# Second FFN of a two-block kernel in two phases, with the up product of a gate and value pair in seven block products

## The chip, the cores and the metric

The kernel runs on one core of a Trainium2 chip. Times are device microseconds of one execution; the median of three runs of the kernel before is 2676.65 us (2674.63 to 2678.04). The engines are PE (TensorE), ACT (ScalarE), DVE (VectorE), POOL (GpSimd) and SP (SyncE, which issues DMAs in order); DMAs that the text calls POOL's are issued in order on POOL's queue.

## What is computed

Two transformer-like blocks run in sequence on x of 1024 tokens by 1024 channels, in float32. The change touches the FFN of the second block (and the loop ahead of it); d_ff is 2816, so the up product has 5632 columns.

```python
    x = x + merged @ w_out[l]
    h2 = _rmsnorm(x, norm2_g[l])
    up = _dwconv_centred(h2 @ w_up[l], ffn_dw_w[l], ffn_dw_b[l])
    gate, val = jnp.split(up, 2, axis=-1)
    x = x + (jax.nn.gelu(gate, approximate=False) * val) @ w_down[l]
return _rmsnorm(x, norm_f_g)
```

The depthwise convolution has three taps along the tokens.

## The kernel before

Activations lie as tiles of 128 channels by 1024 tokens. Each float32 operand is split into a rounded part hi and a rest lo (`split`: ACT makes hi, DVE subtracts), and each product of two tiles is three matmuls, hi by hi, hi by lo and lo by hi, of 128x512. Weights come by `w_prep` in the order of the list `seq`: SP loads wraw (512 KB), ACT makes whi, DVE wlo; there are two buffers of each. The matmuls of one 512-token half add up in one PSUM bank, a tile pg, and `evac` reads it.

**First FFN** (lines 140 to 214 and 806 to 850). Four units of the up product are plain, then `strassen` takes the units in pairs: with four factors T1 to T4 of the activations, made once by `factors`, a pair is 7 block products of 12 matmuls in place of 8 (84 matmuls for 96). `st_prep` makes the weight side of a pair: it loads the first unit as raw, the two halves of the second as U[1] and A, adds U[0] = U[1] + A on DVE, subtracts raw to get V and U[1] = raw - V, and splits S2, S1, S3, A22 and S4 into sh (ACT) and sl (DVE). `keep` copies a partial sum from PSUM to a tile abc on ACT, `ends` (on DVE) adds it to a bank and scales. The result goes to DRAM and is loaded again for the down product, a phase of its own.

**Second block.** In `merge` the eight out2 units (24 matmuls per half, two halves) make x2, DVE adds the residual, `split` makes h2, and `sumsq` adds squares on POOL (line 311). `stats_rB` sums them by two matmuls into pss (line 315) and makes rB, 1/rms per token. `block2_ffn` then runs up unit by up unit: `up(i)` makes the gate unit i and the value unit 22+i, each 48 matmuls, `evac` multiplies by rB on DVE (line 1008), and DVE does the convolution: middle tap and bias (line 1012), two outer taps (1013, 1014); ACT does gelu (1016), DVE the product (1017), and `split` makes the act. The 22 acts are taken in six groups `G2`; the down product of a group (`down`, line 750: x[m] += pg on DVE) runs after the first pairs of the next group. There are three PSUM banks for pg. The last group runs with the final norm.

The order on each engine is made by a scheduler from the program's order; pieces under `high_priority` go earlier, and a pool's buffers set who waits.

Of the kernel before, what the change touches and what calls it, by code (L numbers as in the profile page):

```python
# [57 lines left out]
LEAD, TRAIL = 4, 2  # L58


class Body:
# [694 lines left out]
    def block1_ffn(self):  # L756
        nc, A = self.nc, self.A
        H0, H1 = self.H0, self.H1
        with self.pool("o1") as o1:
# [46 lines left out]

            def factors(j):

                x, y = xr[j], xr[j + 4]
                for t, m in ((x, j), (y, j + 4)):  # L810
                    nc.scalar.activation(out=t, in_=t, func=AF.Copy, scale=self.vec("g_mlp", m))
                a, b = slice(0, HN), slice(HN, T)
# [593 lines left out]
```

## Time and profile before

| | us |
|---|---|
| median of 3 runs | 2676.65 |
| the profiled execution | 2674.9 |
| its span | 2673.1 |
| PE busy | 2619.5 (98%) |
| DVE busy | 1626.0 (61%) |
| ACT busy | 889.4 (33%) |
| POOL busy | 190.0 (7%) |

The granted clock of PE is 0.994 of full speed in the mean. The second FFN with its down product takes PE from about 1940 to 2615 us of the span; the block products of the first FFN stand from 603 to 868 us. The page divides the span into 40 slices of 67 us; the DMA engines are busy 1 to 3 tenths in most of them.

### The profile page before, as it was taken

What the parts mean: (1) busy time and instruction counts of PE and PEld (TensorE: products, weight loads), DVE (VectorE), ACT (ScalarE), POOL (GpSimd) and SP (SyncE); (2) the same over time, 40 slices, a digit from 0 to 9 for tenths busy, and PEclk for the clock granted to TensorE, in tenths of its full rate; (3) what the DMA queues carried; (4) which work ended last, traced back from release to release, by engine and by line L of the source; (5) the groups of instructions that cost most, each with busy time, mean ns of one, the idle gap of its engine ahead of it and who ended that gap; (6) DMA issues with size and microseconds to landing.
All of it is one profiled execution on the core that took longest, in us unless ns stands there. A gap on an engine that the chain in (4) does not pass through costs nothing. (4 is left out here: it accounts for less than half of the span.)

```text
span 2673.1 us, 31765 instructions
## 1 busy us (share of the span) xinstructions
PE 2619.5 (98%) x12844; PEld 2170.0 (81%) x12844; DVE 1626.0 (61%) x2242; ACT 889.4 (33%) x1307; POOL 190.0 (7%) x175
## 2 busy tenths in 40 slices
PE   8999998999999999999999999999999999999998
PEld 7888886877888888888877778887888888888887
DVE  8688688555655544445398777434566645555664
ACT  5455454334443212124344342413221111111121
POOL 1111111210000000003000000011200000000001
PEclk9999999999999999999999999999999999999999
DMA  3101111323333811124222211112211111111111
GB/s 136 44 29 44 40 44 64 133 99 100 120 101 122 319 49 54 48 97 140 79 82 69 68 49 50 47 49 70 96 40 48 52 51 48 48 48 48 48 63 64
DMA packets 77249, 200.33 MB, mean 75 GB/s; under 512 B 9568, under 2 KB 26288, under 8 KB 77104
## 3 DMA queue, kind: packets, MB, share of 16 engines
q1 hardware_dynamic: 63872, 168.34, 19.1%
q10 hardware_dynamic: 9216, 16.78, 1.7%
q0 software_dynamic: 4016, 13.19, 1.3%
q8 instruction: 101, 1.65, 0.3%
q14 instruction: 44, 0.36, 0.0%
HBM read 164.20 MB, written 34.08 MB: 74 GB/s over the span
## 5 line engine op out<-in xcount | busy, mean ns | idle before, releaser
L217 PE MATMUL pg<-hi,whi 128*128 128x512 f32 (+1 forms) x2576 | 1002.0, 389 | 2.6 <-ACT hi L278 1.9
L217 PE MATMUL pg<-lo,whi 128*128 128x512 f32 (+1 forms) x2576 | 999.2, 388 | 0.8 <-DVE lo L279 0.8
L217 PE MATMUL pg<-hi,wlo 128*128 128x512 f32 (+1 forms) x2576 | 999.0, 388 | 0.3 <-DVE wlo L120 0.3
L217 PEld LDWEIGHTS pg<-hi,whi 128*128 128x128 f32 x2576 | 484.6, 188 | 101.8 <-ACT hi L278 2.3
L217 PEld LDWEIGHTS pg<-lo,whi 128*128 128x128 f32 x2576 | 484.6, 188 | 99.0 <-issue 1.2
L217 PEld LDWEIGHTS pg<-hi,wlo 128*128 128x128 f32 x2576 | 484.6, 188 | 97.4 <-DVE wlo L120 0.8
L119 ACT ACTIVATE whi<-wraw 128x1024 fp32r<-128x1024 f32 x189 | 200.2, 1060 | 803.1 <-PE pg L217 669.5
L120 DVE TENSOR_TENSOR wlo<-wraw,whi 128x1024 fp32r<-128x1024 f32 x189 | 235.9, 1249 | 85.0 <-ACT whi L119 83.9
L750 DVE TENSOR_TENSOR xr<-xr,pg 128x512 f32<-128x512 f32 x128 | 87.4, 686 | 159.6 <-PE pg L217 159.6
L1008 DVE TENSOR_TENSOR u<-pg,rB 128x512 f32<-128x512 f32 x88 | 60.7, 690 | 176.2 <-PE pg L217 176.2
L1136 DVE SCALAR_TENSOR_TENSOR cv<-u,vecs,cv 128x1023 f32<-128x1023 f32 (+14 forms) x120 | 152.6, 1272 | 1.7
L243 PE MATMUL pg<-hi,whi 128*128 128x512 f32 x256 | 108.5, 424 | 0.0
L750 DVE TENSOR_TENSOR x<-x,pg 128x512 f32<-128x512 f32 x80 | 54.7, 686 | 86.7 <-PE pg L217 86.7
L160 PE MATMUL pg<-hi,sh 128*128 128x512 f32 x260 | 101.7, 391 | 4.1 <-ACT sh L145 4.1
L243 PE MATMUL pg<-hi,wlo 128*128 128x512 f32 x256 | 102.3, 400 | 0.0
L160 PE MATMUL pg<-hi,sl 128*128 128x512 f32 x260 | 101.9, 392 | 0.4 <-DVE sl L126 0.4
L243 PE MATMUL pg<-lo,whi 128*128 128x512 f32 x256 | 101.9, 398 | 0.0
L160 PE MATMUL pg<-lo,sh 128*128 128x512 f32 x260 | 101.7, 391 | 0.0
L278 ACT ACTIVATE hi<-c 128x1024 fp32r<-128x1024 f32 x22 | 23.3, 1061 | 128.0 <-DVE c L1017 128.0
L519 POOL TENSOR_TENSOR X<-bq,b 128x256 f32<-128x256 f32 x60 | 50.5, 855 | 210.3 <-DVE bq L519 93.7
L1268 PEld LDWEIGHTS pao<-V,pT 128*128 128x128 f32 x384 | 48.6, 191 | 20.2 <-ACT pT L1266 16.0
L575 PEld LDWEIGHTS psc<-X 128*128 128x128 f32 x480 | 59.3, 191 | 4.3 <-issue 1.4
(327 smaller groups left out, 3542.6 us busy)
## 6 DMA issues: line engine op xcount, KB each, us to landing
wraw<-w_up SPq DMA_DIRECT2D x63, 512.0 KB, 3.3
wraw<-w_dn SPq DMA_DIRECT2D x54, 512.0 KB, 3.3
wraw<-w_in SPq DMA_DIRECT2D x52, 512.0 KB, 3.4
ad<-r ACTq DMA_DIRECT2D x64, 256.0 KB, 2.1
r<-ad SPq DMA_DIRECT2D x32, 512.0 KB, 6.6
bt<-bias SPq DMA_DIRECT2D x48, 192.0 KB, 2.4
wraw<-w_out SPq DMA_DIRECT2D x16, 512.0 KB, 3.5
wraw<-w_v SPq DMA_DIRECT2D x10, 512.0 KB, 3.8
```

Source lines behind the costliest of these rows:

```text
L119: nc.scalar.activation(out=hi, in_=raw, func=AF.Copy)
L120: nc.vector.tensor_tensor(out=lo, in0=raw, in1=hi.bitcast(F32), op=ALU.subtract)
L160: nc.tensor.matmul(out=p, lhsT=a[:, k, :], rhs=b, start=first and k == 0 and j == 0, stop=k == 3 and j == 2, skip_group_check=True)
L217: nc.tensor.matmul(out=p, lhsT=w, rhs=x[:, hs], start=(i == 0 and j == 0), stop=(i == n - 1 and j == 2))
L243: nc.tensor.matmul(out=p, lhsT=w[:, k, :], rhs=x[:, hs], start=(k == 0 and j == 0), stop=(k == 7 and j == 2))
L278: nc.scalar.activation(out=hi, in_=src, func=AF.Copy)
L519: tt = lambda e, o, a, b, op: e.tensor_tensor(out=o, in0=a, in1=b, op=op)
L575: nc.tensor.matmul(out=ps[:, j, :], lhsT=lt[:, js], rhs=r, start=True, stop=True)
L750: nc.vector.tensor_tensor(out=xr[m][:, hs], in0=xr[m][:, hs], in1=p, op=ALU.add)
L1008: nc.vector.tensor_tensor(out=u[:, hs], in0=p, in1=self.rB[:, hs], op=ALU.mult)
L1136: nc.vector.scalar_tensor_tensor(out=c[:, o], in0=u[:, s], scalar=w(k), in1=c[:, o], op0=ALU.mult, op1=ALU.add)
L1268: nc.tensor.matmul(out=po[0][:, n, ps_], lhsT=pT[:, kt, :], rhs=V[h + kt][:, n, ps_], start=(kt == 0), stop=(kt == 2))
```

## The change

The eight out2 units run in the order 0, 4, 1, 5, ... (`PAIRED`), each stores its x2 to DRAM (x2d, tile xe) on POOL's queue. The second FFN becomes two phases. Up: three plain pairs (gate i and value 22+i), then pairs 3 to 20 by `strassen` with the gate as first and the value as second unit, then pair 21 plain inside strassen's `tail`. Each act goes to DRAM (ad2, tile ae) by SP. Down: all groups, with acts and x2 loaded again by SP. `factors` is a method now and makes T1 to T4 of the second FFN beside the first two leading pairs. Six PSUM banks serve pg in both phases, three the last group. In `conv3` the middle tap is an activation on ACT (Identity with scale and bias). With `wsb = (1, 3, True)` the second FFN's `st_prep` has one buffer of U and A (the first FFN two), three of sh, sl and abc (four), and two sums by DMA: U[0] is loaded with one half by SP and POOL's queue adds the other half to it from DRAM; lo is set to -hi by ACT and POOL's queue adds raw to it from DRAM.

```diff
 LEAD, TRAIL = 4, 2
+LEAD2, TRAIL2 = 3, 1
...
-        U = ws.tile([P, 2, HN], F32, tag="U", name=self.nm("U"), bufs=2)
-        A = ws.tile([P, HN], F32, tag="A", name=self.nm("A"), bufs=2)
+        nu, ns, summed = self.wsb
+        U = ws.tile([P, 2, HN], F32, tag="U", name=self.nm("U"), bufs=nu)
+        A = ws.tile([P, HN], F32, tag="A", name=self.nm("A"), bufs=nu)
         V = ws.tile([P, 2, HN], F32, tag="V", name=self.nm("V"), bufs=1)
         nc.sync.dma_start(out=raw, in_=a1)
         nc.sync.dma_start(out=U[:, 1, :], in_=a2[:, 0:HN])
         nc.sync.dma_start(out=A, in_=a2[:, HN:D])
-        nc.scalar.activation(out=hi, in_=raw, func=AF.Copy)
-        tt(lo, raw, hi.bitcast(F32), ALU.subtract)
-        tt(U[:, 0, :], U[:, 1, :], A, ALU.add)
+        if summed:
+
+            nc.sync.dma_start(out=U[:, 0, :], in_=a2[:, 0:HN])
+            nc.gpsimd.dma_start(out=U[:, 0, :], in_=a2[:, HN:D], accum_op=ALU.add)
+            nc.scalar.activation(out=hi, in_=raw, func=AF.Copy)
+            nc.scalar.activation(out=lo, in_=hi.bitcast(F32), func=AF.Copy, scale=-1.0)
+            nc.gpsimd.dma_start(out=lo, in_=a1, accum_op=ALU.add)
+        else:
+            nc.scalar.activation(out=hi, in_=raw, func=AF.Copy)
+            tt(lo, raw, hi.bitcast(F32), ALU.subtract)
+            tt(U[:, 0, :], U[:, 1, :], A, ALU.add)
...
-            sh = ws.tile([P, HN], F32R, tag="sh", name=self.nm("sh"), bufs=4)
-            sl = ws.tile([P, HN], F32R, tag="sl", name=self.nm("sl"), bufs=4)
+            sh = ws.tile([P, HN], F32R, tag="sh", name=self.nm("sh"), bufs=ns)
+            sl = ws.tile([P, HN], F32R, tag="sl", name=self.nm("sl"), bufs=ns)
...
+    def factors(self, j, xr, g, pool, TA, TB):
+
...
-            t = self.ws.tile([P, HN], F32, tag="abc", name=self.nm("abc"), bufs=4)
+            t = self.ws.tile([P, HN], F32, tag="abc", name=self.nm("abc"), bufs=self.wsb[1])
...
-        seq += [(("out2", m), A["w_out2"][m]) for m in range(8)]
-        pair = lambda i: [(("up2", i), A["w_up2"][i]), (("up2", 22 + i), A["w_up2"][22 + i])]
+        seq += [(("out2", m), A["w_out2"][m]) for m in PAIRED]
+        up2 = lambda r: [(("up2", j), A["w_up2"][j]) for i in r for j in (i, 22 + i)]
+        seq += up2(range(LEAD2))
+        seq += [(("st", i), (A["w_up2"][i], A["w_up2"][22 + i])) for i in range(LEAD2, 22 - TRAIL2)]
+        seq += up2(range(22 - TRAIL2, 22))
         for g, (a, b) in enumerate(self.G2):
-            if g == 0:
-                for i in range(a, b):
-                    seq += pair(i)
...
-        with self.psum(PG[3]), self.pool("c2") as c2:
+        with self.pool("c2") as c2:
             self.c2 = c2
-            self.merge(cs, attn)
-            self.block2_ffn()
+            with self.psum(PG[3]):
+                self.merge(cs, attn)
+            with self.psum(6):
+                TA, TB = [], []
+                for i in range(LEAD2):
+                    self.up2(i, self.t4, 1 if i < LEAD2 - 1 else 0)
+                    for j in ((0, 1), (2, 3))[i] if i < 2 else ():
+                        self.factors(j, self.x2, "g_n2", H1, TA, TB)
+        self.block2_ffn(TA, TB)
...
-        for m in range(8):
+        for m in PAIRED:
             xi = self.t4("xi")
             nc.sync.dma_start(out=xi, in_=self.xbd[m])
...
-            self.h2.append(self.split(H0, x, self.vec("g_n2", m)))
+            self.h2[m] = self.split(H0, x, self.vec("g_n2", m))
+            nc.gpsimd.dma_start(out=self.x2d[m], in_=x)
             self.sumsq(self.t4, acc, x, m == 0)
...
+    def conv3(self, j, u, c):
+        nc = self.nc
+        w = lambda k: self.vec("fw", 3 * j + k)
+        nc.scalar.activation(out=c, in_=u, func=AF.Identity, scale=w(1), bias=self.vec("fb", j))
+        nc.vector.scalar_tensor_tensor(out=c[:, 1:], in0=u[:, :-1], scalar=w(0), in1=c[:, 1:], op0=ALU.mult, op1=ALU.add)
+        nc.vector.scalar_tensor_tensor(out=c[:, :-1], in0=u[:, 1:], scalar=w(2), in1=c[:, :-1], op0=ALU.mult, op1=ALU.add)
+        if j < 22:
+            self.gelu = nc.scalar.activation(out=c, in_=c, func=AF.Gelu)
+        return c
+
+    def gated(self, i, cg, cv):
+        nc = self.nc
+        nc.vector.tensor_tensor(out=cv, in0=cv, in1=cg, op=ALU.mult)
+        nc.sync.dma_start(out=self.ad2[i], in_=cv)
...
+        self.wsb = (1, 3, True)
+        with self.psum(6), self.pool("ws2") as self.ws:
+            u, c = tag(self.ws, "u", 3), tag(self.ws, "c", 2)
+            us, cs = {}, {}
+
+            def ends(key, r, h, p, a):
+
+                i = key[1]
+                hs = slice(h * HN, h * HN + HN)
+                k = (i, r)
+                whole = k in us
+                t = us[k] = us[k] if whole else u("u")
+                src = p
+                if a is not None:
+                    nc.vector.tensor_tensor(out=t[:, hs], in0=p, in1=a, op=ALU.add)
+                    src = t[:, hs]
+                nc.vector.tensor_tensor(out=t[:, hs], in0=src, in1=self.rB[:, hs], op=ALU.mult)
+                if whole:
+                    with self.tc.high_priority(offset=-HP_EVAC):
+                        cs[k] = self.conv3(22 * r + i, us.pop(k), c("c"))
+                        if (i, 1 - r) in cs:
+                            self.gated(i, cs.pop((i, 0)), cs.pop((i, 1)))
+
+            def tail():
+                two = lambda n: (u if n == "u" else c)(n)
+                self.up2(22 - TRAIL2, two)
+            self.strassen([("st", i) for i in range(LEAD2, 22 - TRAIL2)], self.right(self.h2, TA, TB), ends, tail)
+        with self.pool("c3") as self.c2:
+            self.down2()
...
+        def load(g):
+            for i in range(*self.G2[g]):
+                r = self.big(H0 if g else H1, F32, "r")
+                nc.sync.dma_start(out=r, in_=self.ad2[i])
+                acts[i] = self.split(H1, r)
+
+        xr = []
+        load(0)
+        for m in range(8):
+            xr.append(self.c2.tile([P, T], F32, tag="mg", name=self.nm("xr"), bufs=8))
+            nc.sync.dma_start(out=xr[m], in_=self.x2d[m])
+        with self.psum(6):
+            for g, (a, b) in enumerate(self.G2[:5]):
+                load(g + 1)
+                self.down([("dn2", g, i) for i in range(4 if g else 2)], b - a, 2 if g else 4, xr,
+                          [acts.pop(k) for k in range(a, b)])
+        with self.psum(3):
+            self.last([acts.pop(k) for k in range(*self.G2[5])], xr)
```

PE at the end of out2, before: the last row of out2 (pg_14783), then rows of the first up unit (pg_14844, 18 in all), then the two pss matmuls.

```order
L217 MATMUL pg_14783<-lo_14260,whi_14683 128x512
L217 MATMUL pg_14783<-hi_14259,wlo_14684 128x512
L217 MATMUL pg_14844<-hi_14328,whi_14752 128x512
L217 MATMUL pg_14844<-lo_14329,whi_14752 128x512
...
L217 MATMUL pg_14844<-lo_14672,whi_14752 128x512
L217 MATMUL pg_14844<-hi_14671,wlo_14753 128x512
L315 MATMUL pss_14817<-acc_14264,ones 128x512
L315 MATMUL pss_14827<-acc_14264,ones 128x512
L217 MATMUL pg_14844<-hi_14740,whi_14752 128x512
```

PE at the same place in the change (pg_14820 is the last out2 unit, pg_14890 the first up unit):

```order
L247 MATMUL pg_14820<-hi_14289,whi_14719 128x512
L247 MATMUL pg_14820<-lo_14290,whi_14719 128x512
L247 MATMUL pg_14820<-hi_14289,wlo_14720 128x512
L345 MATMUL pss_14855<-acc_14294,ones 128x512
L345 MATMUL pss_14865<-acc_14294,ones 128x512
L247 MATMUL pg_14890<-hi_14358,whi_14789 128x512
L247 MATMUL pg_14890<-lo_14359,whi_14789 128x512
```

The 18 matmuls of the up unit now stand behind pss.

SP at the start of the block products in the change (ae is the store of an act, U and A the halves of a second unit's weights; before, SP had only wraw loads here):

```order
L1026 DMA ae_92<-c_15006 128x1024
L135 DMA wraw_15332<-w_up 128x1024
L135 DMA wraw_15368<-w_up 128x1024
L1026 DMA ae_93<-c_15163 128x1024
L1026 DMA ae_94<-c_15314 128x1024
L136 DMA U_15335<-w_up 128x512
L137 DMA A_15336<-w_up 128x512
L140 DMA U_15335<-w_up 128x512
```

The first loads of U and A stand behind the store of the third leading pair's act, ae_94.

DVE in the second FFN before, one value unit (u, wlo, taps c, product, lo):

```order
L1008 TENSOR_TENSOR u_15437<-pg_15444,rB_14816 128x512
L1008 TENSOR_TENSOR u_15437<-pg_15470,rB_14816 128x512
L1012 TENSOR_SCALAR c_15496<-u_15437,vecs 128x1024
L120 TENSOR_TENSOR wlo_15508<-wraw_15506,whi_15507 128x1024
L1013 SCALAR_TENSOR_TENSOR c_15496<-u_15437,vecs,c_15496 128x1023
L1014 SCALAR_TENSOR_TENSOR c_15496<-u_15437,vecs,c_15496 128x1023
L1017 TENSOR_TENSOR c_15496<-c_15496,c_15432 128x1024
L1008 TENSOR_TENSOR u_15505<-pg_15512,rB_14816 128x512
L279 TENSOR_TENSOR lo_15502<-c_15496,hi_15501 128x1024
L1008 TENSOR_TENSOR u_15505<-pg_15538,rB_14816 128x512
```

DVE in one unit of the block products in the change, from V to the split of S4, sl<-U with U_16078 (three rows of the fifteen left out):

```order
L127 TENSOR_TENSOR V_16080<-U_16078,wraw_16075 128x1024
L1060 TENSOR_TENSOR u_16221<-pg_16111,rB_14854 128x512
L127 TENSOR_TENSOR U_16078<-wraw_16075,V_16080 128x512
L127 TENSOR_TENSOR sl_16092<-V_16080,sh_16091 128x512
...
L1018 SCALAR_TENSOR_TENSOR c_16290<-u_16221,vecs,c_16290 128x1023
L1060 TENSOR_TENSOR u_16306<-u_16306,rB_14854 128x512
L1058 TENSOR_TENSOR u_16157<-pg_16112,abc_16193 128x512
L127 TENSOR_TENSOR sl_16100<-V_16080,sh_16099 128x512
L1060 TENSOR_TENSOR u_16157<-u_16157,rB_14854 128x512
L127 TENSOR_TENSOR sl_16104<-A_16079,sh_16103 128x512
L1017 SCALAR_TENSOR_TENSOR c_16323<-u_16157,vecs,c_16323 128x1023
L127 TENSOR_TENSOR sl_16108<-U_16078,sh_16107 128x512
```

The units' weight sums, two evacuations by an addition and a product, and two convolutions stand between one unit's V and its last use of U.

SP at the end of the block products in the change (r is the load of an act, xr that of x2):

```order
L1082 DMA r_18903<-ae_107 128x1024
L1082 DMA r_18909<-ae_108 128x1024
L1026 DMA ae_112<-c_18124 128x1024
L1082 DMA r_18915<-ae_109 128x1024
L1082 DMA r_19169<-ae_110 128x1024
L1089 DMA xr_18167<-xe_84 128x1024
L1089 DMA xr_18169<-xe_85 128x1024
```

DVE there; the last row is followed by the first addition to xr, which is the first evacuation of the down product:

```order
L1025 TENSOR_TENSOR c_18105<-c_18105,c_18041 128x1024
L309 TENSOR_TENSOR lo_18210<-r_18207,hi_18209 128x1024
L309 TENSOR_TENSOR lo_18356<-r_18353,hi_18355 128x1024
L1017 SCALAR_TENSOR_TENSOR c_18124<-u_17979,vecs,c_18124 128x1023
L309 TENSOR_TENSOR lo_18362<-r_18359,hi_18361 128x1024
L1018 SCALAR_TENSOR_TENSOR c_18124<-u_17979,vecs,c_18124 128x1023
L1017 SCALAR_TENSOR_TENSOR c_18142<-u_17915,vecs,c_18142 128x1023
L1018 SCALAR_TENSOR_TENSOR c_18142<-u_17915,vecs,c_18142 128x1023
L1025 TENSOR_TENSOR c_18124<-c_18124,c_18142 128x1024
L776 TENSOR_TENSOR xr_18167<-xr_18167,pg_18219 128x512
```

The first load of xr stands behind the store of unit 20's act, ae_112, whose product is the last row.

## Rows read from the trace of the kernel before

**Rows 1.** The page: busy us (share of the span) and instructions of each engine.

```profile
PE 2619.5 (98%) x12844; PEld 2170.0 (81%) x12844; DVE 1626.0 (61%) x2242; ACT 889.4 (33%) x1307; POOL 190.0 (7%) x175
```

**Rows 2.** Windows: stretch, us, busy us of PE, PEld, DVE, ACT, POOL, PEclk, DMA, GB/s.

```profile
1990.00:2400.00 410.00, 409.31 (x1804) 337.94 (x1803) 233.04 (x250) 67.94 (x64) 0.00 (x0) 1.00 0.15 49
603.20:867.90 264.70, 260.24 (x1142) 214.65 (x1140) 153.98 (x213) 109.50 (x175) 0.00 (x0) 0.99 0.34 111
867.90:1228.00 360.10, 360.10 (x1594) 298.32 (x1593) 177.93 (x207) 88.38 (x87) 19.48 (x13) 1.00 0.32 116
```

**Rows 3.** Groups by line, 1990 to 2400 us: count | busy us, mean ns | idle before.

```profile
L1014 DVE SCALAR_TENSOR_TENSOR c<-u,vecs,c 128x1023 f32<-128x1023 f32 x26 | 33.4, 1283 | 0.8
...
L1012 DVE TENSOR_SCALAR c<-u,vecs 128x1024 f32<-128x1024 f32 x26 | 21.1, 812 | 0.9
...
L1017 DVE TENSOR_TENSOR c<-c,c 128x1024 f32<-128x1024 f32 x13 | 15.9, 1224 | 0.3
...
L1016 ACT ACTIVATE c<-c 128x1024 f32<-128x1024 f32 x13 | 13.8, 1061 | 56.6 <-DVE c L1014 56.6
```

**Rows 4.** Groups by line in the block products of the first FFN.

```profile
L145 ACT ACTIVATE sh<-U 128x512 fp32r<-128x512 f32 x26 | 16.2, 625 | 25.5 <-PE pg L160 25.5
L126 DVE TENSOR_TENSOR V<-U,wraw 128x1024 f32<-128x1024 f32 x13 | 15.9, 1225 | 0.4
...
L126 DVE TENSOR_TENSOR U<-U,A 128x512 f32<-128x512 f32 x13 | 9.0, 691 | 11.0 <-DMA U<-w_up 11.0
```

**Rows 5.** Timeline of DVE in the second FFN: start us, us, instruction.

```profile
2006.53 1.28 DVE L1014 SCALAR_TENSOR_TENSOR c<-u,vecs,c 128x1023 f32<-128x1023 f32 x1
2007.72 0.68 DVE L750 TENSOR_TENSOR x<-x,pg 128x512 f32<-128x512 f32 x1
2008.32 1.22 DVE L1017 TENSOR_TENSOR c<-c,c 128x1024 f32<-128x1024 f32 x1
```

**Rows 6.** Timeline of PE at three gaps: idle time before, in brackets.

```profile
559.77 3.78 PE L315 MATMUL pss<-acc,ones 128*128 128x512 f32 x4 [3.47 <-POOL acc L311]
...
613.01 0.50 PE L160 MATMUL pg<-hi,sh 128*128 128x512 f32 x1 [4.10 <-ACT sh L145]
...
1938.90 1.98 PE L315 MATMUL pss<-acc,ones 128*128 128x512 f32 x4 [1.52 <-POOL acc L311]
```

**Rows 7.** Windows at and behind these gaps, columns as in rows 2.

```profile
565.00:566.00 1.00, 1.00 (x4) 0.80 (x3) 1.00 (x2) 0.61 (x1) 0.00 (x0) 0.62 0.00 0
...
613.00:614.00 1.00, 0.79 (x2) 0.30 (x2) 1.00 (x2) 1.00 (x3) 0.00 (x0) 0.77 0.00 0
...
616.00:617.00 1.00, 1.00 (x4) 0.78 (x3) 1.00 (x1) 0.17 (x1) 0.00 (x0) 0.52 0.25 82
...
1936.00:1944.00 8.00, 6.48 (x26) 4.38 (x25) 2.01 (x3) 4.41 (x6) 2.60 (x1) 1.00 0.18 66
```

**Rows 8.** Instructions of line 281, by form: ns min/median/max, first and last start.

```profile
L281 ACT ACTIVATE hi<-x,vecs x8: 1136/1138/1139, 1858.0 to 1934.1; 128x1024 fp32r<-128x1024 f32 x8
```

**Rows 9.** Timeline of DVE at the last out2 evacuation.

```profile
1933.34 0.69 DVE L990 TENSOR_TENSOR x<-pg,xi 128x512 f32<-128x512 f32 x1 [3.45 <-PE pg L217]
```

**Rows 10.** DMA issues: count, KB each, median us from issue to landing.

```profile
xd<-xr POOLq DMA_DIRECT2D x8, 512.0 KB, 3.2
xr<-xd SPq DMA_DIRECT2D x8, 512.0 KB, 7.1
...
U<-w_up SPq DMA_DIRECT2D x13, 256.0 KB, 3.3
A<-w_up SPq DMA_DIRECT2D x13, 256.0 KB, 4.0
...
yd<-y POOLq DMA_DIRECT2D x8, 256.0 KB, 2.6
...
bd<-pool_w POOLq DMA_DIRECT2D x4, 16.0 KB, 5.8
```

**Rows 11.** Timeline of SP's queue in the block products of the first FFN.

```profile
714.48 0.33 SPq L134 DMA_DIRECT2D U<-w_up  x1
```

More of the change, by code (lines that the diff above doesn't have):

```diff
@@ L149, in st_prep, with right @@
         self.wready.append((key, W, None))
+    def factors(self, j, xr, g, pool, TA, TB):
+        nc = self.nc
+        x, y = xr[j], xr[j + 4]
+        for t, m in ((x, j), (y, j + 4)):
+            nc.scalar.activation(out=t, in_=t, func=AF.Copy, scale=self.vec(g, m))
+        a, b = slice(0, HN), slice(HN, T)
+        sub = lambda o, p, q: nc.vector.tensor_tensor(out=o, in0=p, in1=q, op=ALU.subtract)
+        sub(y[:, b], x[:, b], y[:, b])
+        sub(x[:, b], x[:, b], x[:, a])
+        sub(x[:, a], x[:, a], y[:, b])
+        sub(y[:, a], y[:, a], x[:, a])
+        TA.append(self.split(pool, x))
+        TB.append(self.split(pool, y))
+    def right(self, h, TA, TB):
+        half = lambda ts, c: [tuple(t[:, c * HN:c * HN + HN] for t in tt) for tt in ts]
+        return dict(B11=half(h[:4], 0), B21=half(h[4:], 0), B22=half(h[4:], 1),
+                    T2=half(TA, 0), T1=half(TA, 1), T4=half(TB, 0), T3=half(TB, 1))
     def strassen(self, keys, R, ends, tail):
@@ L805, in block1_ffn @@
             TA, TB = [], []
[L807 to L812, printed above, removed]
-                sub = lambda o, p, q: nc.vector.tensor_tensor(out=o, in0=p, in1=q, op=ALU.subtract)
-                sub(y[:, b], x[:, b], y[:, b])
-                sub(x[:, b], x[:, b], x[:, a])
-                sub(x[:, a], x[:, a], y[:, b])
-                sub(y[:, a], y[:, a], x[:, a])
-                TA.append(self.split(H0, x))
-                TB.append(self.split(H0, y))
             for i in range(LEAD):
@@ L823, in block1_ffn @@
                 for j in ((0, 1), (2, 3))[i] if i < 2 else ():
-                    factors(j)
+                    self.factors(j, xr, "g_mlp", H0, TA, TB)
+        self.wsb = (2, 4, False)
         with self.pool("ws") as self.ws:
-            half = lambda ts, c: [tuple(t[:, c * HN:c * HN + HN] for t in tt) for tt in ts]
-            R = dict(B11=half(h[:4], 0), B21=half(h[4:], 0), B22=half(h[4:], 1),
-                     T2=half(TA, 0), T1=half(TA, 1), T4=half(TB, 0), T3=half(TB, 1))
+            R = self.right(h, TA, TB)
             def ends(key, i, c, p, a):
@@ new lines, in gated, with up2, evac @@
+    def gated(self, i, cg, cv):
+        nc = self.nc
+        nc.vector.tensor_tensor(out=cv, in0=cv, in1=cg, op=ALU.mult)
+        nc.sync.dma_start(out=self.ad2[i], in_=cv)
+    def up2(self, i, tile, ahead=1):
+        nc = self.nc
+        c = []
+        for j in (i, 22 + i):
+            u = tile("u")
+            def evac(h, hs, p):
+                nc.vector.tensor_tensor(out=u[:, hs], in0=p, in1=self.rB[:, hs], op=ALU.mult)
+            self.unit(("up2", j), self.h2, evac, ahead=1 if j < 22 else ahead)
+            c.append(self.conv3(j, u, tile("c")))
+        self.gated(i, *c)
@@ L997, in block2_ffn @@
+    def block2_ffn(self, TA, TB):
         nc, A = self.nc, self.A
         H0, H1 = self.H0, self.H1
[L999 to L1018 removed]
@@ L1020, in block2_ffn @@
-        for g, (a, b) in enumerate(self.G2):
-            if g == 0:
-                for i in range(a, b):
-                    up(i)
-            nx = list(range(*self.G2[g + 1])) if g < 5 else []
-            n1 = 4 if g == 4 else 1
-            for i in nx[:n1]:
-                up(i)
-            act = [acts.pop(k) for k in range(a, b)]
-            if g < 5:
-                self.down([("dn2", g, i) for i in range(4 if g else 2)], b - a, 2 if g else 4, xr, act)
-            for i in nx[n1:]:
-                up(i)
+        tag = lambda pool, t, n: lambda name: pool.tile([P, T], F32, tag=t, name=self.nm(name), bufs=n)
@@ L1034, in block2_ffn, with last @@
+    def last(self, act, xr):
+        nc, A = self.nc, self.A
+        H0, H1 = self.H0, self.H1
         w = [tuple(t.rearrange("p (m k c) -> p m k c", m=2, k=4) for t in self.w_get(("dn2", 5, i), ahead=min(WA, 3 - i))) for i in range(4)]
```

34 lines of the change are left out of this document (7 added, 27 removed).

## The prediction

> **What bounds the kernel now.** I read the page's busy times first: PE is busy for 98% of the span, DVE for 61% [rows 1]. That is an average, so I went to the stretch that the change rewrites, with the busy times by window: of 410 us inside the second FFN, PE is busy for 409.31 with 1804 matmuls, that is 0.2269 us per matmul of 128x512, at a granted clock of 1.00 (2.4 GHz), and DVE for 233 [rows 2]. Nothing waits there except the others for PE, so every matmul that is left out gives its 0.227 us, as long as PE stays the bound. The first FFN already runs its up product in seven block products: its stage (second row) has PE busy for 260.24 of 264.70 us, and the down product behind it (third row) for all of its 360.10 us. This shows that the scheme can keep PE fed, with U and A in two buffers and the sums on DVE; the new one has one buffer of each, sums by DMA, and more work per unit on DVE. The groups by line give the prices [rows 3, 4], the timeline the pitch of DVE [rows 5], and three gaps of PE with their granted clock show what a stall costs [rows 6, 7].
>
> **The matmuls.** 18 pairs go from 96 to 84 matmuls of the same shape: 216 fewer, x 0.2269 = **-49.0 us**. A pair takes PE 19.05 us for 21.8. The down product, the three leading pairs and the last one keep their number.
>
> **DVE and ACT.** The middle tap leaves DVE (44 x 0.812 = 35.7 us) and goes to ACT; two of a unit's sums leave too (1.22 for lo, priced as the gate product of the same size, and 0.69 for U). A unit on DVE is then one V (1.225), four outer taps (1.28), one gate product (1.22) and 13 operations on 512 columns (0.69) [rows 3, 4]. Independent operations start 0.09 apart less than they last (1.19 for 1.28, 0.60 for 0.68) [rows 5], so this is 1.13 + 4.8 + 1.13 + 7.8 = 14.9 us, some 16 with waits: below 19.05. DVE in sum is not the bound. ACT has 68 of 410 us busy [rows 2] and room for all of it, the negated copy of hi (1.06) of each unit too. I price the tap on ACT at 1.14, an activation with a pointer operand on 1024 columns [rows 8]; it counts only where a chain runs through it (+0.3 at either end of the stage). The page "ScalarE: Activation LUTs" of the Trainium skill (Rules for kernel authors) says that add and mul belong on VectorE, up to three times faster there in bf16; the rows give 1.14 against 0.81 in f32, and the move would still be hidden, so it changes the two chains by 0.3 us each. The four rounds of factors (DVE 4 subtractions of 0.69 and two splits, ACT four operations) lie beside the last out2 units and the lead pairs, where DVE waits for PE most of the time (3.45 us ahead of one evacuation [rows 9]); without that cover they would cost some 20 us of DVE, none of PE. The stores of x2 and of the acts, and their loads, are cheap on queues that are otherwise waiting, but their places on SP are the matter of the next three terms.
>
> **The end of out2.** Before, 18 matmuls of the first up unit stand between out2's last matmul and the two pss matmuls; now none does. The chain behind the last out2 matmul goes from DVE's evacuation at 1933.34 over ACT's square and POOL's sum to pss at 1938.90 [rows 6, 9]: 5.6 us, of which 18 x 0.2269 = 4.08 was covered and 1.52 was idle. Now it is bare, with a split of T ahead of it on ACT: 5.9, so **+4.4 us**. A gap of 3.47 us at the same point of the first FFN left the granted clock at half (0.50, 1.2 GHz) from PE's return at 559.8 until 565.8 (0.62 in that slice) [rows 6, 7]: half of 6.0 us is lost, **+3.0**; the 1.52 gap left the clock at 1.00. Bounds: 0 (ACT free early) and 9.
>
> **The start of the block products.** The first unit's U and A have no reason of their own to wait, but stand on SP behind the store of the third leading pair's act. From PE's last lead matmul: evacuation 0.69, tap on ACT 1.14, two taps 1.28 each, gate product 1.22, with handovers 5.8; the issues of 0.33 [rows 11] and the landing of 3.3 [rows 10] make 10.3; the accumulation 3.8 (below), V 1.23 and sh 0.63 give 16.1 with handovers. PE has A11 and A12 for 24 x 0.227 = 5.4: **10.7 us idle**, where the first FFN lost 4.10 [rows 6], where the results are stored from ACT's queue and nothing on SP stands ahead of the loads. The clock there was at half from 613.5 to 617.0 (0.77 and 0.52 in the first and last slice) [rows 7], 1.7 us lost: **+12.4** in all. Bounds 4.1 + 1.7 (like the first FFN) and 15.
>
> **The loop through U.** This is the term that decides. U has one buffer. The last reader of a unit's U is sl of S4 on DVE; then SP loads both halves of the next, POOL's DMA adds to the one, DVE makes V, and 14 more operations of DVE later stands the next sl of S4. On DVE that is V 1.13, three taps 3.6, eleven of 0.60, 6.6: 11.3, and about 1.0 of waits, of which 0.7 is the tap on ACT (0.69 + 1.14 + 0.05 behind the product that it needs, less the two operations of 0.60 in between): 12.3. The load: the second issue 0.33 after the first [rows 11] and a landing of 3.3 for U, 4.0 for A in front of it [rows 10]; as both halves go out at once I take 3.8, so 4.2 with the handover. **The accumulating DMA has no row.** Below it is a plain POOL store of 256 KB, 2.6; above, the slowest kind on that queue, 5.8 for 16 KB in small pieces [rows 10]; a plain store of twice the bytes takes 3.2, and a sum that reads source and target moves that much. I take 3.8, a little above it, since the queue carries another sum of 512 KB for each unit. Period: 12.3 + 4.2 + 3.8 = 20.3 us against PE's 19.05, x 17 units: **+21.3 us** (bounds 0 and 55). Idle of 1.25 us per unit is below the 1.52 that left the clock up, so none is added for it.
>
> The Trainium skill's page "Collectives: The Full Stack" (The bandwidth ceiling) says that an add in the DMA path needs two source reads and so pushes twice the traffic; "DMA: Bandwidth & Descriptors" prices a transfer on GpSimd's queue at 2.0 us + bytes/436e3. By these a sum over 256 KB would take an estimated 3.2 and the loop would cost 11 us, 10 less than in my sum. The row of 2.6 agrees with that formula for a plain 256 KB; no row shows an accumulation.
>
> **The end of the block products.** The first xr load stands on SP behind the store of unit 20's act, and the first xr addition on DVE behind its gate product. After PE's last product, DVE has before that: an addition and a product (0.6, 0.7), five taps (1.19 each, the last 1.28), three splits and a gate product (1.13 each), gelu (1.06) to wait for and the last gate product (1.22): 14.6 with handovers. Then four issues and a landing between 3.3 and 7.1 [rows 10]; with two 512 KB loads just ahead 4.7: the load lands 20.6 after PE's last product. PE can fill six banks meanwhile, 6 x 6 x 0.227 = 8.2. With the addition of 0.68: **13.1 us idle, +14.8** with the clock's 1.7. Bounds 0 (as in the first FFN, whose down product starts without a gap) and 18.
>
> **Sum.** -49.0 + 7.4 + 12.4 + 21.3 + 14.8 = **+6.9 us** on the profiled execution's 2674.9 (span 2673.1): 2681.8. The median of the runs shown stands 1.75 higher, which makes 2683.5. A measurement tells about 0.2%, 5.4 us.
>
> **Rivals.**
> - *The loop closes in time.* If the load lands after 3.3 and the sum costs what a plain store does, the loop is 12.3 + 3.7 + 2.6 = 18.6, below 19.05: PE bounds, the term of 21.3 goes. It decides where load and sum together stay under 6.75 us. The sum is then -14.4: 2662. For it: the transfers are small and the DMA share in this stretch is 0.15 [rows 2]. Against it: nothing is left over, any collision with the 512 KB loads breaks it.
> - *The sum is dear.* At 5.8, the row of bd, the loop is 22.3, +55.3: in all +40.9, 2717.5. For it: that queue's loads, small as they are, took longest. Against it: its stores of 256 and 512 KB took about half of that.
> - *Both ends are covered* as in the first FFN: start 4.1 + 1.7, end 0, loop as I forecast: -49.0 + 7.4 + 5.8 + 21.3 = -14.5, 2662. Against it: the places on SP and DVE, where the waiting rows stand one behind the other.
> - *The full gain*, PE never waiting: 2628. It needs all of the above to be hidden; I give it nothing of its own.
>
> **How the numbers follow.** Forecast 0.42 (own range 2668 to 2698, a sum of 3 to 4.7 us; slower 0.25, same 0.10, faster 0.07). Loop in time 0.28 (faster 0.22, same 0.06). Dear sum 0.20, all slower. Ends covered 0.10 (faster 0.08, same 0.02). That makes faster 0.37, same 0.18, slower 0.45. The range reaches from 2656, rival one with 6 us less at the ends, to 2717.5, the dear sum at its bound.
>
> **What would show it.** PE's matmuls fall by 216. In the stage of the block products DVE waits once per unit at V for the DMA into U, sh of S2 comes late, and PE idles some 1.25 us at S2. If PE's busy share there is over 98%, rival one holds; if a unit takes over 21.5 us, rival two. The accumulating DMA's median to landing decides between them. Ahead of the stage PE must show one gap of about 6 us released by POOL's acc, one of about 11 released by sh, and behind it one of about 13 released by DVE's first xr addition, each with the clock at 0.50 behind it. The prediction is wrong in its reasons if the V's wait is for DVE itself or for PE, or if the gaps are elsewhere.

## The result and the profile after

The changed kernel takes 2709.07 us (median of 4 runs, 2706.34 to 2712.04), the kernel before, run beside it, 2677.35: a ratio of 1.012, 95% interval 1.0103 to 1.0138. It is slower by some 32 us; 2683.5 was forecast. The profiled execution takes 2706.34 us with a span of 2704.6, 31.4 and 31.5 more than before.

The page of the changed kernel, the row that answers to [rows 1]:

```profile
PE 2593.3 (96%) x12628; PEld 2131.4 (79%) x12628; DVE 1682.7 (62%) x2366; ACT 1031.6 (38%) x1513; POOL 226.0 (8%) x219
```

PE has its 216 matmuls less and is busy for 26 us less, yet the span is longer: its waits have grown by more. What PE waited for, by line (us in total, times, longest):

```profile
PE pg L190 <- ACT sh L155: 19.2, 4, 12.7
PE pg L247 <- DVE xr L776: 16.3, 1, 16.3
PE pg L190 <- ACT abc L196: 15.4, 26, 1.2
PE pss L345 <- POOL acc L341: 13.0, 2, 9.5
```

Three long waits stand there, as forecast (the sums at sh and pss also hold the first FFN's waits of 4.1 and 3.5), and 26 short ones put down to ACT's abc. Lines 190 and 345 are the block products and pss, 247 every plain unit, 776 the addition to xr. The windows behind the three gaps and in the steady part of the block products, columns as in [rows 2]:

```profile
1948.00:1949.00 1.00, 1.00 (x5) 0.77 (x5) 0.69 (x1) 0.99 (x2) 0.00 (x0) 0.89 0.00 0
2036.00:2038.00 2.00, 2.00 (x8) 1.57 (x8) 0.63 (x1) 1.83 (x3) 0.87 (x1) 0.76 0.00 0
2079.60:2353.40 273.80, 258.15 (x1093) 202.06 (x1093) 198.74 (x248) 124.24 (x170) 22.81 (x27) 1.00 0.47 125
2460.00:2461.00 1.00, 1.00 (x5) 0.77 (x5) 1.00 (x2) 0.21 (x1) 0.00 (x0) 0.89 0.02 8
```

From the slices at 1948, 2036 and 2460 the clock came back to full at 1948.1, 2037.0 and 2460.2; until then it was at half, as in [rows 7]. In the steady stretch it stays at 1.00, but PE is busy for only 258.15 of 273.80 us. That is 0.236 us for each of its 1093 matmuls, for 0.227 before: part of the time lost counts as busy, so the table below takes the loop's cost from the starts of V.

| term | forecast | measured |
|---|---|---|
| 216 matmuls | -49.0 | -49.0 |
| end of out2: idle, clock | +4.4, +3.0 | +8.0, +2.7 |
| start of the block products | +10.7, +1.7 | +12.7, +3.0 |
| loop through U, 17 units | +21.3 | +35.1 |
| end of the block products | +13.1, +1.7 | +16.3, +3.1 |
| sum | +6.9 | +31.9 |

The measured sum is 0.5 from the difference of the profiled executions, so whatever else changed comes to no more than that in sum. The idle times are the brackets in the fences below (9.50 less the 1.52 of before), the clock's part is half the time from PE's return to full clock. For the loop: the 18 starts of V run from 2028.97 to 2387.91, 21.11 us per unit, less PE's 19.05, x 17.

**The loop.** One turn in the timelines of DVE, SP and POOL:

```profile
2196.86 1.23 DVE L127 TENSOR_TENSOR V<-U,wraw 128x1024 f32<-128x1024 f32 x1 [3.67 <-DMA U<-w_up]
...
2208.44 0.68 DVE L127 TENSOR_TENSOR sl<-U,sh 128x512 fp32r<-128x512 f32 x1
...
2209.14 0.33 SPq L136 DMA_DIRECT2D U<-w_up  x1
2209.53 0.52 SPq L140 DMA_DIRECT2D U<-w_up  x1
...
2213.44 0.88 POOL L141 DMA_DIRECT2D U<-w_up  x1 [7.21 <-DVE u L1058]
...
2217.61 1.23 DVE L127 TENSOR_TENSOR V<-U,wraw 128x1024 f32<-128x1024 f32 x1 [3.56 <-DMA U<-w_up]
```

From V at 2196.86 to the end of the last split of U at 2209.12 are 12.3 us; the loads of U go out 0.02 later, and POOL issues its sum at 2213.44, 4.3 after that split and 3.9 after the second load went out (the bracket names the last event on DVE before it, an operation whose result the sum doesn't read); V starts at 2217.61, 4.2 later, after a wait of 3.56 for that DMA. Over the 17 turns the three legs are 12.43, 4.54 and 4.14 in the mean. The DMA issues (count, KB each, median us to landing) have the price that had no row:

```profile
wlo<-w_up POOLq DMA_DIRECT2D x18, 512.0 KB, 5.4
...
U<-w_up POOLq DMA_DIRECT2D x18, 256.0 KB, 4.1
...
xr<-xe SPq DMA_DIRECT2D x8, 512.0 KB, 8.7
```

256 KB added by DMA take 4.1 us, 512 KB 5.4; a plain store of 256 KB takes 2.6 [rows 10]. The Trainium skill's formula for that queue ("DMA: Bandwidth & Descriptors", Anatomy of one DMA), with twice the bytes by the two reads of "Collectives: The Full Stack" (The bandwidth ceiling), gives an estimated 3.2 and 4.4: both are 0.9 to 1.0 short here.

**The three gaps.** Ahead of pss (DVE, POOL, PE):

```profile
1935.29 0.68 DVE L1006 TENSOR_TENSOR x<-pg,xi 128x512 f32<-128x512 f32 x1
...
1938.16 1.28 DVE L312 SCALAR_TENSOR_TENSOR lo<-x,vecs,hi 128x1024 fp32r<-128x1024 f32 x1
1939.36 1.22 DVE L309 TENSOR_TENSOR lo<-x,hi 128x1024 fp32r<-128x1024 f32 x1
1940.70 2.61 DVE L168 TENSOR_TENSOR x<-x,x 128x512 f32<-128x512 f32 x1
...
1938.19 4.58 POOL L341 TENSOR_TENSOR acc<-acc,sq 128x1024 f32<-128x1024 f32 x1 [1.36 <-ACT sq L340]
...
1942.82 1.22 PE L345 MATMUL pss<-acc,ones 128*128 128x512 f32 x1 [9.50 <-POOL acc L341]
```

The last evacuation starts at 1935.29, not 1933.34 [rows 9], behind splits of T; POOL's addition takes 4.58 us, not 2.6. At the start (SP, POOL, DVE, PE):

```profile
2018.68 0.33 SPq L1026 DMA_DIRECT2D ae<-c  x1
...
2020.16 0.72 SPq L140 DMA_DIRECT2D U<-w_up  x1
...
2025.29 0.87 POOL L141 DMA_DIRECT2D U<-w_up  x1 [8.40 <-DMA U<-w_up]
...
2028.97 1.22 DVE L127 TENSOR_TENSOR V<-U,wraw 128x1024 f32<-128x1024 f32 x1 [8.99 <-DMA U<-w_up]
...
2030.91 0.79 PE L190 MATMUL pg<-hi,sh 128*128 128x512 f32 x1 [12.73 <-ACT sh L155]
```

The store stands where it was read to stand; U's second load is issued at 2020.16, and POOL's sum on it goes out 5.1 us later, at 2025.29. At the end (DVE, SP, PE):

```profile
2443.00 1.23 DVE L1025 TENSOR_TENSOR c<-c,c 128x1024 f32<-128x1024 f32 x1 [1.18 <-ACT c L1020]
2453.32 1.97 DVE L776 TENSOR_TENSOR xr<-xr,pg 128x512 f32<-128x512 f32 x3 [9.09 <-DMA xr<-xe]
...
2445.98 5.07 SPq L1089 DMA_DIRECT2D xr<-xe  x7
...
2454.06 0.79 PE L247 MATMUL pg<-hi,whi 128*128 128x512 f32 x1 [16.33 <-DVE xr L776]
```

DVE is through with the gate product at 2444.2, the load of xr goes out at 2445.98 and has landed at 2453.3.

### The profile page after: what moved, and what is told of

It is laid out like the page before. It is cut to its first block, busy times and chain, and to the rows that moved or that the text cites. A ratio compares the mean times of both kernels' runs of the same rounds, so it can differ in the third digit from the quotient of the medians.

```text
span 2704.6 us, 32029 instructions
## 1 busy us (share of the span) xinstructions
PE 2593.3 (96%) x12628; PEld 2131.4 (79%) x12628; DVE 1682.7 (62%) x2366; ACT 1031.6 (38%) x1513; POOL 226.0 (8%) x219
## 5 line engine op out<-in xcount | busy, mean ns | idle before, releaser
L247 PE MATMUL pg<-hi,whi 128*128 128x512 f32 (+1 forms) x2000 | 779.9, 390 | 18.9 <-DVE xr L776 16.3
L247 PE MATMUL pg<-lo,whi 128*128 128x512 f32 (+1 forms) x2000 | 776.6, 388 | 0.8 <-DVE lo L309 0.8
L247 PE MATMUL pg<-hi,wlo 128*128 128x512 f32 (+1 forms) x2000 | 776.1, 388 | 0.3 <-DVE wlo L121 0.3
L247 PEld LDWEIGHTS pg<-hi,whi 128*128 128x128 f32 x2000 | 377.4, 189 | 95.7 <-DVE xr L776 16.7
L190 PE MATMUL pg<-hi,sh 128*128 128x512 f32 x620 | 248.0, 400 | 35.2 <-ACT sh L155 19.2
L190 PE MATMUL pg<-hi,sl 128*128 128x512 f32 x620 | 245.1, 395 | 2.4 <-DVE sl L127 2.2
L190 PE MATMUL pg<-lo,sh 128*128 128x512 f32 x620 | 244.0, 394 | 0.0
L190 PEld LDWEIGHTS pg<-hi,sh 128*128 128x128 f32 x620 | 117.6, 190 | 73.5 <-ACT abc L196 29.0
L190 PEld LDWEIGHTS pg<-hi,sl 128*128 128x128 f32 x620 | 117.8, 190 | 32.9 <-DVE sl L127 8.4
L190 PEld LDWEIGHTS pg<-lo,sh 128*128 128x128 f32 x620 | 117.8, 190 | 23.6
```

The costliest lines, as they stand in the source:

```text
L190: nc.tensor.matmul(out=p, lhsT=a[:, k, :], rhs=b, start=first and k == 0 and j == 0, stop=k == 3 and j == 2, skip_group_check=True)
L247: nc.tensor.matmul(out=p, lhsT=w, rhs=x[:, hs], start=(i == 0 and j == 0), stop=(i == n - 1 and j == 2))
```

## The experiments

**Is it the loop, and which part of it?** Four edits of the changed kernel, e1 to e4. First (e1), U[0] and U[1] as two tiles, which come free apart; the load of U[0] also goes to the head of the three on SP, and V is made by two operations:

```diff
-        U = ws.tile([P, 2, HN], F32, tag="U", name=self.nm("U"), bufs=nu)
+        if summed:
+            U0 = ws.tile([P, HN], F32, tag="U0", name=self.nm("U0"), bufs=nu)
+            U1 = ws.tile([P, HN], F32, tag="U1", name=self.nm("U1"), bufs=nu)
...
+            tt(V[:, 0, :], U0, raw[:, 0:HN], ALU.subtract)
+            tt(V[:, 1, :], U1, raw[:, 0:HN], ALU.subtract)
```

> U[0] and U[1] become two tiles of one buffer each (V is made by two operations of 512 columns in place of one of 1024); both sums stay on DMA. In the changed kernel a unit of the block products takes 21.1 us by V's starts: 12.5 from V to the end of the last split of U on DVE, 4.3 until the load of U has landed, 4.2 for the sum by DMA. Theory (the loop through the one buffer of U sets the pace): U[0] is free after the split of S1, 8 us before U[1], so its load and sum leave the loop and 12.5 + 0.6 + 4 = 17 us is left, below PE's 19.05. A unit takes 19.1 to 19.8, V's wait for the DMA into U is gone or below 1 us, and the run takes 2674 to 2685. Rival (PE waits for ACT, which the profile names with abc behind most of PE's gaps in the loop; ACT's order of whi, wlo, sh and abc sets the pace): the period stays at 20.5 to 21.1, the run at 2699 to 2709.

Measured: 2670.63 us (ratio to the kernel before 0.9972, 0.9961 to 0.9983), 38 less than the change and below the theory's range: the loop's whole cost went, and the gap ahead of the stage fell too, from 12.73 to 10.44. Both DMA sums are still there and U's still takes 4.1; PE waits for abc in 2 places for 1.6 us in all, for 15.4 in 26 before. So what the profile put down to ACT was the loop: the engine named last in a chain need not be its cause.

Second (e2), the sum in U on DVE:

```diff
-            nc.sync.dma_start(out=U[:, 0, :], in_=a2[:, 0:HN])
-            nc.gpsimd.dma_start(out=U[:, 0, :], in_=a2[:, HN:D], accum_op=ALU.add)
+            tt(U[:, 0, :], U[:, 1, :], A, ALU.add)
```

> The sum U[0] = U[1] + A goes back to DVE, lo stays a sum by DMA; one buffer of U and A. Theory of the loop: one load of 3.9 and an addition of 0.6 in place of 8.5 of DMA, 12.5 + 3.9 + 0.6 = 17 us: PE sets the pace, 19.1 to 19.8 per unit, 2674 to 2685. Rival (ACT's order): ACT does the same work, 20.5 or more, 2699 to 2709. Second rival (DVE is full): 0.6 more per unit on it makes it slower, 2709 to 2720.

Measured: 2665.93 (0.9956, 0.9942 to 0.9970), 43 less than the change and again below the theory's range; the first gap fell to 8.27. V no longer waits for a DMA, its starts are 19.04 apart in the steady stretch, and PE is never idle there:

```profile
2060.00:2340.00 280.00, 280.00 (x1237) 231.86 (x1236) 238.93 (x296) 153.44 (x192) 12.20 (x14) 1.00 0.38 110
```

Third (e3), lo on DVE:

```diff
-            nc.scalar.activation(out=lo, in_=hi.bitcast(F32), func=AF.Copy, scale=-1.0)
-            nc.gpsimd.dma_start(out=lo, in_=a1, accum_op=ALU.add)
+            tt(lo, raw, hi.bitcast(F32), ALU.subtract)
```

> lo goes back to DVE (raw minus hi), the sum in U stays on DMA. Theory of the loop: lo's split stands between V and the last split of U on DVE, so the loop grows by 1.1 us a unit, less what the DMA into U gains by having the queue alone (0 to 0.6): 0.5 to 1.1 x 17, 2718 to 2728. Rival (ACT's order): ACT loses 1.04 us per unit that stood ahead of sh and abc, so a unit gets shorter by 0.5 to 1.0: 2692 to 2700.

Measured: 2707.77 (1.0110, 1.0095 to 1.0125), the change's time. Neither side's number came: the leg on DVE grew by 0.4 to 12.87, the load's shrank by as much to 4.12, the sum's took 4.36. The leg grew by so little because lo's split of 1.1 us fills the 0.7 to 0.9 that DVE had waited for ACT's tap; in most turns that wait is gone. ACT has 1.04 us less per unit and nothing got faster, which speaks against ACT's order once more; the DMA for lo is not in the loop.

Fourth (e4), the middle tap on DVE:

```diff
-        nc.scalar.activation(out=c, in_=u, func=AF.Identity, scale=w(1), bias=self.vec("fb", j))
+        nc.vector.tensor_scalar(out=c, in0=u, scalar1=w(1), scalar2=self.vec("fb", j), op0=ALU.mult, op1=ALU.add)
```

> The middle tap goes back to DVE, in all 44 units. Theory of the loop: between V and the last split of U stand now two taps of 0.73 and two outer taps of 1.19 (one outer tap falls behind the split), 11.6 in place of 12.5, and the wait for ACT's tap is gone: a unit takes 20.1 to 20.5, 2692 to 2702. Rival (ACT's order): ACT loses 2.5 us per unit, PE's waits for abc go, a unit takes 19.1 to 19.5, 2674 to 2682. Second rival (DVE is full): 1.5 more per unit, 21.5 or more, 2716 or more.

Measured: 2712.81 (1.0129, 1.0114 to 1.0144), 4 more than the change. My count missed: the leg on DVE takes 12.82 in the mean, not 11.6, 21.5 per unit in all. Two outer taps were counted in it, and in 14 of the 17 turns three stand there (one at 2232.05, 2235.83 and 2238.47), which makes 13.0 to 13.25. The rival with ACT is refuted here too: PE still waits 14.7 us for abc. DVE full is not it either, though 21.5 per unit is that rival's number: V waits for U's DMA in every unit (80.7 us in all, 74.6 in the change).

**The gaps**, on top of the sum in U on DVE (2666). First (e5), merge and the leading pairs in one pool of three banks:

```diff
                 self.merge(cs, attn)
-            with self.psum(6):
                 TA, TB = [], []
```

> As e2_usum_dve (2666), and the leading pairs share merge's pool of three PSUM banks, so that 21 matmuls of the first up unit stand ahead of the two pss matmuls again, and DVE's subtractions for T stand behind pss. Theory (the gap of 9.45 us ahead of pss is a bare chain, with 2.0 us of it from POOL's last addition taking 4.6 for 2.6 us while DVE runs those subtractions): 4.8 is covered and the addition is back at 2.6, a gap of 2.5 to 3.5 is left and the granted clock loses half as much or nothing; 2657 to 2661. Rival (the gap is set by DVE's four splits of T ahead of the evacuation alone): POOL's addition still takes 4.6, a gap of 4.5 to 5 is left, 2661 to 2663.

Measured: 2661.16 (0.9943, 0.9930 to 0.9957). POOL, DVE and PE ahead of pss:

```profile
1942.04 4.57 POOL L340 TENSOR_TENSOR acc<-acc,sq 128x1024 f32<-128x1024 f32 x1 [1.36 <-ACT sq L339]
...
1942.00 1.28 DVE L311 SCALAR_TENSOR_TENSOR lo<-x,vecs,hi 128x1024 fp32r<-128x1024 f32 x1
1943.19 1.23 DVE L308 TENSOR_TENSOR lo<-x,hi 128x1024 fp32r<-128x1024 f32 x1
...
1946.67 1.09 PE L344 MATMUL pss<-acc,ones 128*128 128x512 f32 x1 [4.71 <-POOL acc L340]
```

The rival holds: 4.7 us are covered, but POOL's addition is as slow as before, with no subtraction of T beside it. DVE has two splits there.

Second (e6), the stores of the leading and of the last two acts on ACT's queue:

```diff
-        nc.sync.dma_start(out=self.ad2[i], in_=cv)
+        (nc.scalar if i < LEAD2 or i >= 20 else nc.sync).dma_start(out=self.ad2[i], in_=cv)
```

> As e2_usum_dve (2666), and the acts of the three leading pairs and of the last two pairs are stored from ACT's queue, not SP's, so that neither the first load of U nor the first load of xr stands behind a store that waits for DVE. Theory (the order on SP is what makes both loads late): the gap at the first S2 goes from 8.3 to 2 to 5 us, the one at the first xr addition from 16.3 to 7 (DVE's gate product of pair 20 still stands ahead of the addition); with the clock 2650 to 2655. Rival (both loads wait for the memory that they take over: U that of the leading pairs' tiles, xr that of the block products' tiles, whatever the order on SP): start 7 to 8.3, end 14 to 16.3, 2662 to 2666.

Measured: 2663.60 (0.9948, 0.9933 to 0.9964). The first gap falls from 8.27 to 5.50, just above what the theory gave; the last only from 16.27 to 14.46. The time and the last gap lie in the rival's ranges. Here are SP and DVE at the end:

```profile
2385.60 14.72 SPq L1081 DMA_DIRECT2D r<-ae  x13
2401.70 12.49 SPq L1088 DMA_DIRECT2D xr<-xe  x7
...
2405.91 1.23 DVE L1024 TENSOR_TENSOR c<-c,c 128x1024 f32<-128x1024 f32 x1 [1.18 <-ACT c L1019]
2410.68 1.28 DVE L775 TENSOR_TENSOR xr<-xr,pg 128x512 f32<-128x512 f32 x2 [3.54 <-DMA xr<-xe]
```

The first xr load now goes out ahead of the gate product (2401.70, 2405.91), and still lands only at 2410.6, behind 13 loads of 512 KB. So neither the store ahead of it on SP nor, for the first load, memory was the whole cause; what is left is the queue of transfers, which e8 below tests.

Both together (e7):

> e5_lead_psum and e6_st_act together. If the three gaps are separate, the gains add: 2641 to 2650. If one waits behind another (the stage starts earlier, but the loads are not there earlier), less than the sum: 2650 to 2657.

Measured: 2658.05 (0.9929, 0.9916 to 0.9941). The gaps are 4.72, 5.50 and 14.45, those of the two runs apart, and the gains add (4.8 and 2.3 from 2665.9 give 2658.8); the range was missed because e6 alone had given less.

Third (e8), the loads of later acts behind the first xr load, by an edge on SP:

```diff
+                if g:
+                    with self.tc.issue_after(first.ins):
+                        nc.sync.dma_start(out=r, in_=self.ad2[i])
...
+            first = d if m == 0 else first
```

> As e7_all (2658), and the loads of acts for all groups but the first stand on SP behind the first load of xr. In e7 and e6 the first xr load is issued 10 us before PE has use for it and lands 9 us later, behind 13 loads of 512 KB; three splits of those acts stand on DVE ahead of the first addition to xr. Theory (the gap of 14.5 us at the first addition is that queue of transfers and those splits): the load lands in 3 to 5 us, DVE's chain from PE's last product is 8.5 to 10 us, a gap of 2 to 6 us is left; with less time at half clock 2645 to 2651. Rival (xr waits for the memory of the last pair's tiles, which pair 20's gate product gives free): the gap stays at 9 to 14.5, 2653 to 2658.

Measured: 2648.60 (0.9891, 0.9873 to 0.9909). PE at the first addition:

```profile
2398.11 0.79 PE L246 MATMUL pg<-hi,whi 128*128 128x512 f32 x1 [6.62 <-DVE xr L775]
```

The median landing of xr falls from 9.8 in e6 to 4.8 us, and the gap from 14.45 to 6.62, a little over the range. The edit takes away two things and does not part them: in e7 DVE waits 3.68 us for the load ahead of the first addition, and three splits of those acts, some 3.4 us, stood in its chain. What is left is DVE's chain, with a wait of 4.46 us for ACT's last tap, which waits for the store that has to leave one of the two c tiles.

Fourth (e9), the factors later:

```diff
-                        self.factors(j, self.x2, "g_n2", H1, TA, TB)
+                        with self.tc.issue_after(self.rb_ins):
+                            self.factors(j, self.x2, "g_n2", H1, TA, TB)
...
+        self.rb_ins = self.rexp.ins
```

> As e8_xr_first, and ACT's share of the factors T1 to T4 is queued behind the last activation of rB, so that no split of T stands on DVE ahead of out2's last evacuation, nor beside POOL's last addition. Theory (the gap of 4.7 us ahead of pss is 2.0 of DVE's splits and 2.0 of POOL's addition taking 4.6 us beside DVE's work): the addition takes 2.6, the gap is 0.5 to 1.5 and the clock stays at 1.00: 6 to 7 us less than e8. Rival (POOL's addition is slow for another reason, as the store of x2 just ahead of it on its queue): it stays at 4.6, the gap at 2.5 to 3, 2 to 4 us less.

Measured: 2645.37 (0.9879, 0.9864 to 0.9895), 3.2 less than e8 by the medians and 6.6 by the two profiled executions' spans. By the medians that is in the rival's range, by the spans in the theory's (e8's profiled execution was the slowest of its four); the rows decide. POOL and PE ahead of pss:

```profile
1937.41 0.57 POOL L1008 DMA_DIRECT2D xe<-x  x1 [6.32 <-DVE x L1005]
1939.35 2.59 POOL L340 TENSOR_TENSOR acc<-acc,sq 128x1024 f32<-128x1024 f32 x1 [1.36 <-ACT sq L339]
...
1941.99 0.70 PE L344 MATMUL pss<-acc,ones 128*128 128x512 f32 x1 [1.52 <-POOL acc L340]
```

The addition is back at 2.59, with the same store of x2 ahead of it, the gap at 1.52 as in [rows 6], and the clock stays up. So what e9 moved away from beside it, not the store, made POOL's addition slow; e5 had shown that two splits are enough.

Fifth (e10), the five stores on POOL's queue:

```diff
-        (nc.scalar if i < LEAD2 or i >= 20 else nc.sync).dma_start(out=self.ad2[i], in_=cv)
+        (nc.gpsimd if i < LEAD2 or i >= 20 else nc.sync).dma_start(out=self.ad2[i], in_=cv)
```

> As e9_factors_late, but the five stores of acts go out on POOL's queue, not ACT's. In e6 and e7 ACT holds a store that waits for DVE's gate product ahead of the first abc, and DVE waits 1.0 for that abc, ahead of V. If that wait is on the path to the first S2 (gap of 5.5 us): 1 to 1.5 us less there, and with the clock 1 to 2 us less than e9. If V waits for DVE's own work: the same as e9 within 1 us.

Measured: 2644.88 (0.9877, 0.9861 to 0.9893): the first gap falls from 5.50 to 4.38, 1.1 as expected; the time can't be told from e9's.

**Did the moves off DVE earn anything?** In e9 with the edit of e4 (e11), and then with that of e3 too (e12):

> As e9_factors_late (2645), and the middle tap back on DVE. In e9 DVE is busy for 239 of 280 us in the block products, 16.3 per unit of 19.04, and PE for all of it. Two taps of 0.73 more make 17.7. Theory (the move of the tap is worth nothing once no load is in the loop; PE sets the pace): a unit stays at 19.04, and the chains at both ends are 0.3 shorter: 2643 to 2647. Rival (DVE's order, not its sum, bounds the unit, and 93% is too full): 19.3 to 20 per unit, 2650 to 2662.

> As e11_tap_dve, and lo back on DVE too, so that no sum is left on DMA and none of the change's three moves off DVE is there. DVE would have 17.7 + 1.13 = 18.8 of 19.05 us. Theory (DVE is full now, and each of its waits for ACT adds to the unit): 19.3 to 20 us per unit, 2650 to 2661. Rival (the waits find cover): 19.05 to 19.2, 2644 to 2648.

Measured: 2646.78 (0.9890, 0.9873 to 0.9906) and 2648.02 (0.9892, 0.9877 to 0.9906). With everything on DVE:

```profile
2060.00:2340.00 280.00, 280.00 (x1237) 231.86 (x1236) 273.82 (x340) 99.96 (x149) 0.00 (x0) 1.00 0.24 87
```

DVE is busy for 273.82 of 280 us, and PE still never waits; the units stay at 19.04. In e11 that is the theory; in e12 the rival, at its upper edge. The 1.4 us of e11 over e9 are no more than the runs scatter; e12's four runs (2646.3 to 2648.5) all lie above e9's (2643.7 to 2646.2), so its 2.7 us may be real. In both the last gap is longer (8.09 and 8.57 for 6.25).

## Why the prediction was right, and where its sizes were off

Direction and mechanism were right, the time within the range, but the forecast of +6.9 was a fifth of the measured. That 2709 lies in the range is in part luck: the forecast's own part of it ended at 2698, the rest up to 2717.5 was there for a dear sum, which did not come, and the chances were 0.45 for slower against 0.37 for faster. Each of the four positive terms was short. The three long gaps and V's wait for the DMA are where they were put; the short idle in the loop is not: it was to stand at S2, released by sh, and stands where the profile names abc (15.4 us in 26 places).

- **The matmuls**: right; e2 shows the 19.04 per unit.
- **The loop through U**, "the term that decides": it does, as e1 and e2 show from two sides (38 and 43 us less than the change). The period was 20.3 by the prediction, 21.11 measured. The legs: DVE 12.3 for 12.43, load 4.2 for 4.54, sum 3.8 for 4.14. Errors of 0.1 to 0.3 us, all of one sign, in a chain in which nothing is covered, 17 times: 13.8 us. The step that failed is the sizing of the legs: "I take 3.8" for the landing and for the sum. The rival "the loop closes in time" needed 6.75 us for load and sum; they took 8.7. The dear sum of 5.8 did not come: it took 4.1, as the rows of the larger transfers on that queue had spoken for.
- **The end of out2**: the chain was priced with DVE free and POOL's addition at 2.6. DVE's splits of T (2.0) and the slowed addition (2.0) were missed; the factors had been put down as covered work, and they were late work ahead of the chain. e5 shows the addition slow beside two splits alone, and e9 takes splits and slow addition away (a gap of 4.68 in e8, 1.52 in e9). The trace of the kernel before had the price, at the same point of the first FFN, where two splits of 1.28 and 1.22 us on DVE lie beside the addition:

```profile
555.22 4.50 POOL L311 TENSOR_TENSOR acc<-acc,sq 128x1024 f32<-128x1024 f32 x1 [1.43 <-ACT sq L310]
```

- **The start**: DVE's chain 5.9 for 5.8, the sum 3.7 for 3.8; what was short is the landing of U, with 5.1 until the sum goes out for 3.3 (three loads went out in a row; that this is the reason is not shown), and the clock's part, taken from a gap of 4.10: 3.0 for 1.7.
- **The end**: DVE's chain took 14.7 (from PE's last product, 2454.06 - 16.33 - 8.2, to 2444.2) for 14.6. The failing step is the landing of xr, "with two 512 KB loads just ahead 4.7": 7.3 was measured, a little above the upper bound of 7.1. e6 and e8 show why: behind the loads of later acts the first xr load took 8.9 us to land (e6), ahead of them 4.1 (e8). The clock's part was 3.1 for 1.7.
- **The tap on ACT**: in the loop DVE waits 0.7 to 0.9 us for it, of which the forecast's leg of 12.3 held 0.7. It took 1.23 us on ACT, for 1.14. Once the loop is gone it is hidden, and e11 shows that on DVE it is hidden too.

The rival "both ends are covered" fell with the gaps. There is no run with two whole buffers of U: a second one of U and A takes 6 KB more per partition, which this stage's tiles don't leave.

## What to carry to other kernels

A buffer that is given back by the last operation of a unit and filled by two transfers in a row makes a loop whose legs add up; count it against the bottleneck's period before any engine's busy time, and round its legs up. Work moved off an engine that isn't the bound (98% busy with all of it, in e12) earned nothing in the steady stretch and 2.7 us at most in all (e9 against e12), while the latency of the DMA that took over U's sum, inside the loop, cost 35 us. With U in two tiles (e1) the same sums by DMA stand outside the loop, and PE is not held up in the steady stretch. Where a phase ends, look at what is ready early (splits and loads for later) and will stand ahead of what is needed first: the four edits at the two ends (matmuls into the gap, stores off the queue of the loads, later loads and later splits behind the urgent ones) were worth 20 us here (e2 to e9), and the kernel with all of them is 1.2% faster than the one before (e9, e10).
